# Strassen's scheme on alternate pairs of rows, extended from four gate products to six and to half of the output projection

## The chip, the cores and the metric

The program runs on one core of one Trainium2 chip, with float32 data in and out. The metric is the device time of one execution in microseconds. For the kernel before, three runs gave 1011.74 to 1012.43 us, with a median of 1012.02 us.

## The reference

One decoder layer on x of 256 rows (time steps) by 2048 channels:

```python
u = x @ w_in                                   # 2048 x 17920 weights
a_q, a_f, a_i, a_g, b_q, b_k, b_v, b_g, c_b, c_c, c_x, c_g, m_a, m_b, m_c = split(u)
o_a = rms_norm(hgrn2(a_q, a_f, a_i)) * g * silu(a_g)      # 256 x 1024
o_b = window_attention(b_q, b_k, b_v) * silu(b_g)         # 256 x 1024
o_c = short_conv(c_b, c_c, c_x) * silu(c_g)               # 256 x 1024
merged = sum(sigmoid(m_i) * (o_i @ w_proj_i) for i in "abc")   # each m_i: 256 x 2048
y = merged @ w_out                             # 2048 x 2048
out = layer_norm(alpha * x + y) * ln_g + ln_b
```

What the change touches are the three gate products `m_a`, `m_b`, `m_c` (each x times a 2048 x 2048 part of `w_in`) and `merged @ w_out`.

## The kernel before

**Products in three passes.** Every float32 weight is split into `hi` (a cast to fp32r, ScalarE = ACT, line 114) and `lo` (the rest, VectorE = DVE, line 115); the activations are split in the same way once. A product of a 128 x 128 block of activations with a 128 x 512 block of weights takes three matmuls: hi x hi, lo x hi, hi x lo (`rows`, lines 141 to 145; `product`, lines 663 to 668).

**A plain product.** `gemm(src, xs, 512, "rows")` computes 256 x 512 outputs. Weights come in granules of 1 MB (four k-tiles of 128 rows x 512 columns) through three `raw` buffers; each half granule (128 x 1024) is one `hi` and one `lo` instruction, from pools of four buffers each, and feeds 12 matmuls. A contraction of 2048 has 16 k-tiles and takes 96 matmuls of 128 x 512.

**Gates in pairs of groups.** `gate_pair` (line 656) computes two groups of 512 columns at once, 256 x 1024 outputs, and goes over the contraction in eight pairs of k-tiles, one 1 MB granule each. `PAIRS = (0, 1, 0, 1, 0, 1, 0, 1)` says which pairs are done by the scheme. A plain pair is 2 k-tiles x 2 column groups x 2 row blocks x 3 = 24 matmuls, fed by two splits. In the other pairs the 2 x 2 x 2 block product is done by the Strassen-Winograd scheme in seven products, 21 matmuls. Their operands are sums and differences: of the activations (`sums_of_x`, line 636, once), and of the weights. The latter are made for each such pair: `w` by lines 691 to 693 (128 x 1024 and twice 128 x 512, DVE), then the splits into `hi`, `lo` (128 x 1024), `hi2`, `lo2` (128 x 512) and `hw`, `lw` (128 x 2048). After the last pair one ACT copy (line 721) and eight 128 x 512 DVE additions (lines 722 to 729) combine eight PSUM banks into the outputs, and two sigmoids follow.

**Order of the stages.** Input products with the three mixers, whose steps (`hgrn`, `attn`) are generators in `tasks` that `pump()` advances between half granules; conv(1) to conv(3); then for each of four column groups a plain gate product `rows512(MA + d)` and the first branch's projection `w_proj_hgrn`; then, for the second and the third branch, twice one `gate_pair` and two projections; then `turn` (line 625), which transposes `merged` on TensorE and splits it into the four tiles `ms`; then the output projection `w_out`, three plain groups, each followed by `residual` (line 773: one 128 x 512 line 774 and two line 777 for each row block); last the fourth group, whose split weights are kept (`parts`) and used first for row block 0 and then for row block 1, so that the layer norm of block 0 runs beside the matmuls of block 1.

**Buffers.** Pool `w8` has 12 buffers of 8 KB a partition, given out as `t8`: `xs` takes 4 until the gates end, then come `yc`, the branch outputs `outs[...]` (2 each), `sums` (2), `w`, and, for every second pair of `gate_pair`, `hw` and `lw`; later `ms` (4), the residual input `xres` (2), `lg`, `lbt`, and `h8`, `l8` (the split weights of the first two granules of the last group, two tiles for each granule). Pool `mgp` takes the place of the mixers' pool after `mixers.close()` and holds one `hw` and one `lw`. PSUM has four banks for accumulators and four for other uses; `gate_pair` takes all eight.

**Order on an engine.** Each engine executes its instructions in an order that is fixed when the program is built, and that order isn't the order of the source: an instruction whose operands and buffers are there may be placed ahead of an earlier one that waits. All loads of weights are issued from SyncE's queue, those of `xres`, `lg` and `lbt` from ACT's.

Of the kernel before, what the change touches and what calls it, by code (L numbers as in the profile page):

```python
# [9 lines left out]
F32 = mybir.dt.float32  # L10
# [6 lines left out]
P = 128  # L17
# [25 lines left out]
AI, AG, MA = 0, 2, 4  # L43
# [7 lines left out]
def hybrid_kernel(ctx, tc, a, out):  # L51
# [27 lines left out]
    def f32(ap):  # L79
        return ap.bitcast(F32)  # L80
# [358 lines left out]
    def attn(hf, q, kz, v, gate):  # L439
# [10 lines left out]
        y = t4([P, 4, T], "yb")  # L450
# [64 lines left out]
        outs["b"].append(t8([P, 4, 2, T], "ob", F32R))  # L515
        split_to(outs["b"][hf], y)


    def conv(u):
# [27 lines left out]
        nc.vector.tensor_mul(out=yc[:, 2 * u : 2 * u + 2], in0=y, in1=h)  # L547

# [47 lines left out]
    for w in range(2):  # L596
        r = slice(64 * w, 64 * w + 64)
        nc.scalar.copy(out=kz[0][r, :, w], in_=kr[r])
        nc.vector.tensor_sub(out=kz[1][r, :, w], in0=kr[r], in1=f32(kz[0][r, :, w]))
    for hf in range(2):  # L600
# [14 lines left out]
        tasks.append(attn(hf, q, kz, vb, gate))  # L615
    for u in range(1, 4):
        conv(u)
# [15 lines left out]
    pairs = [p for p in range(KT // 2) if PAIRS[p]]  # L633
    sums = []

    def sums_of_x():
        n = len(pairs)
        xr = rawp.tile([P, n, 2, T], F32, tag="raw", name="xr")
        for i, p in enumerate(pairs):
            nc.sync.dma_start(out=xr[:, i], in_=a["xT"][:, 2 * p : 2 * p + 2])  # L640
        x11, x21 = xr[:, :, 0, :P], xr[:, :, 0, P:]
        x12, x22 = xr[:, :, 1, :P], xr[:, :, 1, P:]
        sx = t8([P, 4, n, P], "sx")
        nc.vector.tensor_add(out=sx[:, 0], in0=x21, in1=x22)
        nc.vector.tensor_sub(out=sx[:, 1], in0=sx[:, 0], in1=x11)
        nc.vector.tensor_sub(out=sx[:, 2], in0=x21, in1=x11)
        nc.vector.tensor_sub(out=sx[:, 3], in0=x12, in1=sx[:, 1])
        yield
        for i in range(0, n, 2):
            dst = t8([P, 2, 4, 2, P], "sums", F32R)  # L650
            sums.append(dst)
            for j in range(2):
                split_to(dst[:, j].rearrange("p s h t -> p s h t"), sx[:, :, i + j])
            yield

    def gate_pair(src):
# [13 lines left out]
        def block(k, t):  # L670
            return [xs[k // 4][:, k % 4, i, t * P : t * P + P] for i in range(2)]
# [3 lines left out]
        for p in range(KT // 2):  # L675
# [28 lines left out]
            i = pairs.index(p)  # L704
            sx = [sums[i // 2][:, i % 2, j] for j in range(4)]
            sx = [[y[:, 0], y[:, 1]] for y in sx]
            k = 2 * p
            end = p == last
            product(p1, block(k, 0), hi[:, :NC], lo[:, :NC], end)
            product(p2, block(k + 1, 0), hi[:, NC:], lo[:, NC:], end)  # L710
            pump()
            product(p6, sx[1], hw[:, 2], lw[:, 2], end)
            product(p7, sx[2], hw[:, 1], lw[:, 1], end)
            product(p5, sx[0], hw[:, 0], lw[:, 0], end)
            product(p3, sx[3], hi2, lo2, end)
            product(p4, block(k + 1, 1), hw[:, 3], lw[:, 3], end)
# [208 lines left out]
```

## Time and profile before

| | us |
|---|---|
| median of three runs | 1012.02 |
| the profiled execution | 1011.4 |
| span of its trace | 1009.6 |
| TensorE (PE) busy | 993.0 (98%) |
| VectorE (DVE) busy | 743.5 (74%) |
| ScalarE (ACT) busy | 541.1 (54%) |
| first of the four `gate_pair` stages starts | 654.5 |
| output projection starts | 907.9 |
| last matmul's result is used | 998.5 |

The profiled execution took 1011.4 us; its trace covers 1009.6 us of that, and 1.8 us lie around it. "Busy" counts the time in which at least one instruction of the engine is recorded; matmuls overlap, so the time that a matmul costs is the distance from its start to the next start, not its recorded duration.

### The profile page before, as it was taken

The numbers are of one execution on the slowest core, as the hardware profiler recorded it, in microseconds if no ns is written. First come the engines' busy times: TensorE is split into PE (matmuls) and PEld (weight loads), VectorE is DVE, ScalarE is ACT, GpSimd is POOL, SyncE is SP. The second block draws the span as 40 slices with busy tenths as digits, with TensorE's granted clock in tenths as the row PEclk, the third lists the DMA queues.
The fourth block names the chain that finished last, engine by engine and source line by source line (L and its number), as shares of the span: only waits on it lengthen the run. The fifth ranks groups of instructions, "written<-read, shape, count | busy, mean of one in ns | idle before, by whom it ended". The sixth has DMA issues, their size and how long they took to land.

```text
span 1009.6 us, 13674 instructions
## 1 busy us (share of the span) xinstructions
PE 993.0 (98%) x5454; PEld 839.3 (83%) x5454; DVE 743.5 (74%) x930; ACT 541.1 (54%) x716; POOL 32.4 (3%) x32
## 2 busy tenths in 40 slices
PE   8999999999999999999999999999999999999995
PEld 5888888888888888888888888888888888887885
DVE  6557889689955777778674554687988889876666
ACT  5545578656654665645554434455555564544341
POOL 1000100210010000000000000000000000000003
PEclk9999999999999999999999999999999999999998
DMA  8755545454455545444456555565655555567442
GB/s 318 256 178 198 187 147 184 151 183 155 168 207 187 188 153 197 163 164 161 167 208 213 204 191 187 205 208 195 216 177 205 208 208 208 183 236 290 173 161 83
DMA packets 30831, 193.67 MB, mean 192 GB/s; under 512 B 3840, under 2 KB 4640, under 8 KB 8752
## 3 DMA queue, kind: packets, MB, share of 16 engines
q1 hardware_dynamic: 28944, 185.90, 52.2%
q10 hardware_dynamic: 1152, 4.72, 1.2%
q0 software_dynamic: 672, 2.20, 0.7%
q8 instruction: 42, 0.69, 0.3%
q14 instruction: 21, 0.17, 0.0%
HBM read 190.68 MB, written 2.12 MB: 191 GB/s over the span
## 4 chain that ended last, share of the span: by engine, by line
PE 97%; DVE 1%; DMA 1%; SPq 0%; ACT 0%; issue 0%
PE acc L151 24%; PE acc L145 13%; PE acc L143 13%; PE acc L144 13%; PE acc L150 12%; PE p L668 5%; PE p L667 5%; PE p L666 5%; DMA raw<-in_w_rows 1%; PE sc L464 1%; PE pvb L507 1%; PE acc L153 1%; PE pT L497 1%; PE lev L390 0%; PE pv L416 0%; PE lev L378 0%
## 5 line engine op out<-in xcount | busy, mean ns | idle before, releaser
L114 ACT CAST hi<-raw 128x1024 fp32r<-128x1024 f32 (+1 forms) x341 | 349.3, 1028 | 348.2 <-PE acc L144 143.4
L115 DVE TENSOR_TENSOR lo<-raw,hi 128x1024 fp32r<-128x1024 f32 (+1 forms) x341 | 404.5, 1194 | 175.0 <-ACT hi L114 173.4
L151 PE MATMUL acc<-xs,hi 128*128 128x512 f32 x1056 | 371.6, 396 | 0.0
L150 PE MATMUL acc<-xs,lo 128*128 128x256 f32 x990 | 278.4, 281 | 0.0
L151 PEld LDWEIGHTS acc<-xs,hi 128*128 128x128 f32 x1056 | 196.9, 188 | 43.5
L150 PEld LDWEIGHTS acc<-xs,lo 128*128 128x128 f32 x990 | 186.8, 189 | 2.3
L143 PE MATMUL acc<-hi,xs 128*128 128x512 f32 (+1 forms) x288 | 110.2, 383 | 2.3 <-ACT hi L114 2.3
L145 PE MATMUL acc<-lo,xs 128*128 128x512 f32 (+1 forms) x288 | 108.8, 379 | 0.4 <-DVE lo L115 0.3
L144 PE MATMUL acc<-hi,xs 128*128 128x512 f32 (+1 forms) x288 | 109.0, 378 | 0.0
L143 PEld LDWEIGHTS acc<-hi,xs 128*128 128x128 f32 x288 | 54.4, 189 | 14.8 <-ACT hi L114 4.4
L145 PEld LDWEIGHTS acc<-lo,xs 128*128 128x128 f32 x288 | 54.1, 188 | 11.5 <-DVE lo L115 1.6
L144 PEld LDWEIGHTS acc<-hi,xs 128*128 128x128 f32 x288 | 54.4, 189 | 9.8
L666 PE MATMUL p<-hi,xs 128*128 128x512 f32 x160 | 62.2, 389 | 0.0
L667 PE MATMUL p<-hi,xs 128*128 128x512 f32 x160 | 62.2, 389 | 0.0
L668 PE MATMUL p<-lo,xs 128*128 128x512 f32 x160 | 62.2, 389 | 0.0
L115 DVE TENSOR_TENSOR lw<-w,hw 128x2048 fp32r<-128x2048 f32 x16 | 36.7, 2293 | 15.0 <-ACT hw L114 15.0
L191 ACT COPY rest<-acc 128x256 f32<-128x256 f32 x66 | 24.1, 372 | 42.2 <-PE acc L151 41.5
L143 PE MATMUL acc<-hi,m 128*128 128x512 f32 (+1 forms) x120 | 45.1, 376 | 1.2 <-ACT hi L114 1.2
L144 PE MATMUL acc<-hi,m 128*128 128x512 f32 (+1 forms) x120 | 45.0, 375 | 0.0
L145 PE MATMUL acc<-lo,m 128*128 128x512 f32 (+1 forms) x120 | 44.9, 376 | 0.1
L667 PEld LDWEIGHTS p<-hi,xs 128*128 128x128 f32 x160 | 30.0, 188 | 6.3
L666 PEld LDWEIGHTS p<-hi,xs 128*128 128x128 f32 x160 | 30.0, 188 | 6.2
(232 smaller groups left out, 1313.1 us busy)
## 6 DMA issues: line engine op xcount, KB each, us to landing
raw<-in_w_cols SPq DMA_DIRECT2D x68, 1024.0 KB, 4.8
raw<-in_w_gate SPq DMA_DIRECT2D x32, 1024.0 KB, 4.8
raw<-in_w_rows SPq DMA_DIRECT2D x28, 1024.0 KB, 4.8
raw<-in_w_out SPq DMA_DIRECT2D x16, 1024.0 KB, 4.9
raw<-in_w_proj_hgrn SPq DMA_DIRECT2D x8, 1024.0 KB, 4.8
raw<-in_w_proj_attn SPq DMA_DIRECT2D x8, 1024.0 KB, 4.8
raw<-in_w_proj_conv SPq DMA_DIRECT2D x8, 1024.0 KB, 4.8
raw<-in_w_rows SPq DMA_DIRECT2D x7, 512.0 KB, 9.2
```

The costliest lines, as they stand in the source:

```text
L114: nc.scalar.copy(out=hi, in_=r)
L115: nc.vector.tensor_sub(out=lo, in0=r, in1=f32(hi))
L143: nc.tensor.matmul(out=acc, lhsT=xk[:, 0, ts], rhs=hi, start=first, stop=False)
L144: nc.tensor.matmul(out=acc, lhsT=xk[:, 1, ts], rhs=hi, start=False, stop=False)
L145: nc.tensor.matmul(out=acc, lhsT=xk[:, 0, ts], rhs=lo, start=False, stop=last)
L150: nc.tensor.matmul(out=acc[:, :T], lhsT=lo, rhs=xk[:, 0], start=False, stop=False)
L151: nc.tensor.matmul(out=acc, lhsT=hi, rhs=xk, start=first, stop=last)
L153: nc.tensor.matmul(out=acc[:, :T], lhsT=lo, rhs=xk[:, 0], start=False, stop=False)
L191: nc.scalar.copy(out=rest[p], in_=acc[p, T:])
L666: nc.tensor.matmul(out=ps, lhsT=x[0], rhs=hi, start=begins, stop=False)
L667: nc.tensor.matmul(out=ps, lhsT=x[1], rhs=hi, start=False, stop=False)
L668: nc.tensor.matmul(out=ps, lhsT=x[0], rhs=lo, start=False, stop=last)
```

## The change

Three places change from plain products to pairs of groups by the scheme. The four plain gate products of the first branch become two calls of `pair_of_groups` (the former `gate_pair`, with the sigmoids moved out and the activations, the sums, the order of the products and the number of spare buffers as arguments). The first two of the four groups of `w_out` become one call, on the transposed `merged`. `turn` makes the sums of `merged` for that. Group 2 of `w_out` stays plain and goes first. `sums_of_x` becomes a task behind the attention. The attention's output stays unsplit in `yb` (one buffer of `w8`), and the outputs of the second and third branch are split ahead of their gates.

```diff
-AI, AG, MA = 0, 2, 4
+AI, AG = 0, 2
...
-        y = t4([P, 4, T], "yb")
+        y = yb[:, 4 * hf : 4 * hf + 4]
...
-        outs["b"].append(t8([P, 4, 2, T], "ob", F32R))
-        split_to(outs["b"][hf], y)
...
+    def block_sums(dst, x11, x12, x21, x22):
+        nc.vector.tensor_add(out=dst[0], in0=x21, in1=x22)
+        nc.vector.tensor_sub(out=dst[1], in0=dst[0], in1=x11)
+        nc.vector.tensor_sub(out=dst[2], in0=x21, in1=x11)
+        nc.vector.tensor_sub(out=dst[3], in0=x12, in1=dst[1])
...
+    yb = t8([P, 8, T], "yb")
...
         tasks.append(attn(hf, q, kz, vb, gate))
+    pairs = [p for p in range(KT // 2) if PAIRS[p]]
+    sums = []
+    tasks.append(sums_of_x())
     for u in range(1, 4):
         conv(u)
     pump(100)
...
-    def turn(m):
+    def turn(m, d):
         dst = t8([P, 4, 2, T], "m", F32R)
         ms.append(dst)
+        if d % 2 == 0:
+            msums.append(t8([P, 2, 4, 2, P], "msums", F32R))
         for i, ps in transpose_pairs([[m[:, t, c * P : c * P + P] for t in range(2)] for c in range(4)], "mT"):
             split_to(dst[:, i : i + 2], ps)
+            if PAIRS[2 * d + i // 2]:
+                raw = mgp.tile([P, 2, T], F32, tag="u", name="mraw")
+                nc.scalar.copy(out=raw, in_=ps)
+                sx = mgp.tile([P, 4, P], F32, tag="one", name="sx")
+                block_sums([sx[:, j] for j in range(4)], raw[:, 0, :P], raw[:, 1, :P], raw[:, 0, P:], raw[:, 1, P:])
+                split_to(msums[d // 2][:, d % 2], sx)
             yield
...
-    def gate_pair(src):
+    def pair_of_groups(src, x, sums, raw_first, spare):
...
-            if pairs.index(p) % 2:
-                hw, lw = t8([P, 4, NC], "hw", F32R), t8([P, 4, NC], "lw", F32R)
-            else:
-                hw = mgp.tile([P, 4, NC], F32R, tag="hw", name="hw")
-                lw = mgp.tile([P, 4, NC], F32R, tag="lw", name="lw")
+            i = pairs.index(p)
+            hw, lw = [t8([P, 4, NC], name, F32R) if i % 2 and n < spare else
+                      mgp.tile([P, 4, NC], F32R, tag=name, name=name) for n, name in enumerate(("hw", "lw"))]
             split_w(w, hw, lw)
...
+            whole = [(p1, block(k, 0), hi[:, :NC], lo[:, :NC]), (p2, block(k + 1, 0), hi[:, NC:], lo[:, NC:])]
+            summed = [(p6, sx[1], hw[:, 2], lw[:, 2]), (p7, sx[2], hw[:, 1], lw[:, 1]), (p5, sx[0], hw[:, 0], lw[:, 0])]
+            rest = [(p3, sx[3], hi2, lo2), (p4, block(k + 1, 1), hw[:, 3], lw[:, 3])]
+            for n, y in enumerate(whole + summed + rest if raw_first or end else summed + rest[::-1] + whole):
+                product(*y, end)
+                if n in (2, 5):
+                    pump()
...
-    for d in range(4):
-        acc = rows512(MA + d)
-        sg = mgp.tile([P, 2, NC], F32, tag="sg", name="sg", bufs=2)
-        for t in range(2):
-            nc.scalar.activation(out=sg[:, t], in_=acc[t], func=AF.Sigmoid)
-        acc = gemm(a["w_proj_hgrn"][d], outs["a"], NC, "rows")
-        for t in range(2):
-            nc.vector.tensor_mul(out=merged[d][:, t], in0=acc[t], in1=sg[:, t])
-    pump(100)
-    for n, (wp, br) in enumerate((("w_proj_attn", "b"), ("w_proj_conv", "c"))):
+    mix = {"b": yb, "c": yc}
+    for n, (wp, br) in enumerate((("w_proj_hgrn", "a"), ("w_proj_attn", "b"), ("w_proj_conv", "c"))):
+        if n:
+            for i in range(2):
+                outs[br].append(t8([P, 4, 2, T], "o" + br, F32R))
+                split_to(outs[br][i], mix[br][:, 4 * i : 4 * i + 4])
         for half in range(2):
-            sg = gate_pair(a["w_gate"][2 * n + half])
...
+            sg = pair_of_groups(a["w_gate"][2 * n + half], xs, sums, n > 0, 2 if n else 1)
+            for y in sg:
+                nc.scalar.activation(out=y, in_=y, func=AF.Sigmoid)
...
-    for n in range(3):
-        acc = gemm(a["w_out"][n], ms, NC, "rows")
+    acc = gemm(a["w_out"][2], ms, NC, "rows")
+    for t in range(2):
+        residual(t, slice(2 * NC, 3 * NC), acc[t])
+    y = pair_of_groups(a["w_out2"][0], ms, msums, False, 0)
+    for n in range(2):
         for t in range(2):
-            residual(t, slice(n * NC, n * NC + NC), acc[t])
+            residual(t, slice(n * NC, n * NC + NC), y[n][:, t])
```

So `spare` is 2 for the second and third branch (as before), 1 for the first (`hw` in two buffers, `lw` in one) and 0 for the output (one `hw`, one `lw`). The weights are the same numbers in another order; as many bytes are loaded.

## Rows read from the trace of the kernel before

**Rows 1.** The page: engine, busy us (share of the span), count of instructions.

```profile
PE 993.0 (98%) x5454; PEld 839.3 (83%) x5454; DVE 743.5 (74%) x930; ACT 541.1 (54%) x716; POOL 32.4 (3%) x32
```

**Rows 2.** The page: chain that ended last, by engine.

```profile
PE 97%; DVE 1%; DMA 1%; SPq 0%; ACT 0%; issue 0%
```

**Rows 3.** PE in order of time, end of the last `gate_pair` (start us, duration).

```profile
878.54 0.39 PE L666 MATMUL p<-hi,xs 128*128 128x512 f32 x1
...
883.07 0.39 PE L668 MATMUL p<-lw,xs 128*128 128x512 f32 x1
883.30 0.39 PE L143 MATMUL acc<-hi,oc 128*128 128x512 f32 x1
```

**Rows 4.** Stretches (us): length, each engine's busy us (instructions), PE clock, DMA.

```profile
500.00:533.00 33.00, 33.00 (x179) 28.40 (x178) 25.46 (x34) 19.07 (x27) 0.00 (x0) 1.00 0.62 218
545.00:654.00 109.00, 109.00 (x483) 90.25 (x482) 56.44 (x50) 47.82 (x49) 0.00 (x0) 1.00 0.55 194
842.20:883.00 40.80, 40.80 (x182) 33.78 (x181) 35.52 (x36) 21.57 (x21) 0.00 (x0) 1.00 0.58 203
883.00:907.90 24.90, 24.90 (x123) 20.54 (x122) 17.55 (x24) 10.70 (x14) 0.00 (x0) 1.00 0.63 233
...
986.90:998.50 11.60, 11.60 (x97) 11.41 (x95) 8.59 (x14) 2.07 (x5) 4.56 (x4) 1.00 0.25 91
```

**Rows 5.** Groups by line and shape: count | busy us, mean ns | idle before.

```profile
L115 DVE TENSOR_TENSOR lo<-raw,hi 128x1024 fp32r<-128x1024 f32 x323 | 392.9, 1223 | 172.9 <-ACT hi L114 171.5
...
L115 DVE TENSOR_TENSOR lw<-w,hw 128x2048 fp32r<-128x2048 f32 x16 | 36.7, 2293 | 15.0 <-ACT hw L114 15.0
L114 ACT CAST hw<-w 128x2048 fp32r<-128x2048 f32 x16 | 30.6, 1913 | 4.6 <-DVE w L693 4.4
...
L691 DVE TENSOR_TENSOR w<-raw 128x1024 f32<-128x1024 f32 x16 | 19.5, 1222 | 0.5 <-DMA raw<-in_w_gate 0.5
...
L115 DVE TENSOR_TENSOR lo<-raw,hi 128x512 fp32r<-128x512 f32 x18 | 12.4, 689 | 2.2 <-ACT hi L114 1.9
...
L692 DVE TENSOR_TENSOR w<-raw,w 128x512 f32<-128x512 f32 x16 | 11.0, 690 | 0.2
...
L430 DVE SCALAR_TENSOR_TENSOR oa<-pv,rs,ga 128x128 f32<-128x128 f32 x16 | 4.3, 344 | 3.6 <-POOL rs L425 3.6
```

**Rows 6.** DVE in order of time, first of the four sums of x.

```profile
515.72 0.69 DVE L644 TENSOR_TENSOR sx<-xr 128x512 f32<-128x512 f32 x1
```

**Rows 7.** DMA issues: queue, count, KB each, median us to landing.

```profile
lbt<-in_ln_b ACTq DMA_DIRECT2D x1, 1024.0 KB, 10.7
```

**Rows 8.** PE in order of time, start of the output projection.

```profile
910.70 1.03 PE L262 MATMUL mT<-ident,merged 128*128 128x128 f32 x8
912.92 0.50 PE L143 MATMUL acc<-hi,m 128*128 128x512 f32 x1 [1.18 <-ACT hi L114]
```

**Rows 9.** DVE in order of time, additions at the end of the last `gate_pair`.

```profile
881.99 1.22 DVE L115 TENSOR_TENSOR lo<-raw,hi 128x1024 fp32r<-128x1024 f32 x1
883.12 0.69 DVE L724 TENSOR_TENSOR sg<-p,u 128x512 f32<-128x512 f32 x1
...
886.11 0.69 DVE L729 TENSOR_TENSOR sg<-p,sg 128x512 f32<-128x512 f32 x1
886.70 2.36 DVE L115 TENSOR_TENSOR lo<-raw,hi 128x1024 fp32r<-128x1024 f32 x2
```

**Rows 10.** DVE in order of time, after the third group of `w_out`.

```profile
977.88 0.74 DVE L777 BATCH_NORM_STATS2 stats<-xres 128x6 f32<-128x256 f32 x2
978.54 0.67 DVE L774 SCALAR_TENSOR_TENSOR xres<-xres,acc 128x512 f32<-128x512 f32 x1
979.13 1.22 DVE L115 TENSOR_TENSOR lo<-raw,hi 128x1024 fp32r<-128x1024 f32 x1
...
987.04 0.69 DVE L774 SCALAR_TENSOR_TENSOR xres<-xres,acc 128x512 f32<-128x512 f32 x1 [6.04 <-PE acc L145]
...
994.94 0.41 DVE L774 SCALAR_TENSOR_TENSOR xres<-xres,acc 128x256 f32<-128x256 f32 x1
```

More of the change, by code (lines that the diff above doesn't have):

```diff
@@ L547, in conv, with sums_of_x @@
         nc.vector.tensor_mul(out=yc[:, 2 * u : 2 * u + 2], in0=y, in1=h)
+    def block_sums(dst, x11, x12, x21, x22):
[3 more added lines that the diff above has]
+        nc.vector.tensor_sub(out=dst[3], in0=x12, in1=dst[1])
+    def sums_of_x():
+        n = len(pairs)
+        xr = rawp.tile([P, n, 2, T], F32, tag="raw", name="xr")
+        for i, p in enumerate(pairs):
+            nc.sync.dma_start(out=xr[:, i], in_=a["xT"][:, 2 * p : 2 * p + 2])
+        sx = t8([P, 4, n, P], "sx")
+        block_sums([sx[:, j] for j in range(4)], xr[:, :, 0, :P], xr[:, :, 1, :P], xr[:, :, 0, P:], xr[:, :, 1, P:])
+        yield
+        for i in range(0, n, 2):
+            dst = t8([P, 2, 4, 2, P], "sums", F32R)
+            sums.append(dst)
+            for j in range(2):
+                split_to(dst[:, j], sx[:, :, i + j])
+            yield
     C = {}
@@ L623, in hybrid_kernel @@
     ms = []
-    def turn(m):
+    msums = []
+    def turn(m, d):
         dst = t8([P, 4, 2, T], "m", F32R)
         ms.append(dst)
+        if d % 2 == 0:
+            msums.append(t8([P, 2, 4, 2, P], "msums", F32R))
         for i, ps in transpose_pairs([[m[:, t, c * P : c * P + P] for t in range(2)] for c in range(4)], "mT"):
             split_to(dst[:, i : i + 2], ps)
-            yield
[L633 to L654, printed above, removed]
-    def gate_pair(src):
+            if PAIRS[2 * d + i // 2]:
[4 more added lines that the diff above has]
+                split_to(msums[d // 2][:, d % 2], sx)
+            yield
+    def pair_of_groups(src, x, sums, raw_first, spare):
         p1, p2, p6, p7 = [accp.tile([P, NC], F32, tag="acc", name=f"p{i}") for i in (1, 2, 6, 7)]
@@ L670, in block @@
         def block(k, t):
-            return [xs[k // 4][:, k % 4, i, t * P : t * P + P] for i in range(2)]
+            return [x[k // 4][:, k % 4, i, t * P : t * P + P] for i in range(2)]
         last = KT // 2 - 1
@@ L697, in gate_pair @@
             split_w(flat[:, 3 * NC :], hi2, lo2)
[L698 to L702 removed]
+            i = pairs.index(p)
+            hw, lw = [t8([P, 4, NC], name, F32R) if i % 2 and n < spare else
+                      mgp.tile([P, 4, NC], F32R, tag=name, name=name) for n, name in enumerate(("hw", "lw"))]
             split_w(w, hw, lw)
[L704 to L706 removed]
+            sx = [[sums[i // 2][:, i % 2, j, m] for m in range(2)] for j in range(4)]
             k = 2 * p
             end = p == last
[L709 to L716, printed above, removed]
[L717 to L718 removed]
+            whole = [(p1, block(k, 0), hi[:, :NC], lo[:, :NC]), (p2, block(k + 1, 0), hi[:, NC:], lo[:, NC:])]
[5 more added lines that the diff above has]
+                    pump()
+        y = [mgp.tile([P, 2, NC], F32, tag="sg", name="sg", bufs=2) for _ in range(2)]
         u = mgp.tile([P, NC], F32, tag="u", name="u")
@@ L744, in hybrid_kernel @@
-    pump(100)
-    for n, (wp, br) in enumerate((("w_proj_attn", "b"), ("w_proj_conv", "c"))):
-        for half in range(2):
-            sg = gate_pair(a["w_gate"][2 * n + half])
-            if br == "c" and not half:
-                for i in range(2):
-                    outs["c"].append(t8([P, 4, 2, T], "oc", F32R))
-                    split_to(outs["c"][i], yc[:, 4 * i : 4 * i + 4])
+        nc.vector.tensor_add(out=y[0][:, 1], in0=p7, in1=u)
+        nc.vector.tensor_add(out=y[1][:, 0], in0=p5, in1=u)
@@ L752, in hybrid_kernel @@
             if br == "c" and half:
-                tasks.extend(turn(merged[d]) for d in range(2))
+                tasks.extend(turn(merged[d], d) for d in range(2))
             for j in range(2):
@@ L903 @@
         "w_out": _weights(i["w_out"][0], NC),
+        "w_out2": _quads(i["w_out"][0][:, : 2 * NC]),
         "lb_param": np.ascontiguousarray(i["lb_param"][0].reshape(8, P).T),
```

32 lines of the change are left out of this document (14 added, 18 removed).

## The prediction

> **What bounds the kernel now.** I read the page's engine list first. PE is busy 98% of the span, DVE 74%, ACT 54% [rows 1]. The reader is to see two candidates there, and that one number settles nothing: overlapping matmuls make a busy PE. The chain of waits, read second, puts 97% on PE [rows 2], so what ends last is a nearly unbroken row of matmuls. Third, PE in order of time: inside a gate pair, and across its end into the next projection, a 128x512 matmul starts every 0.227 us (878.54 to 883.07 us holds 21 of them, 20 steps of 0.2265), although each is recorded with 0.39 [rows 3]. The last matmul of the pair and the first of the projection are 0.23 apart as well: the additions and sigmoids between them cost PE nothing, because halves of the next weights had been split before [rows 9]. So the price of a matmul is 0.227 us, and a matmul less is 0.227 us less, as long as the splits come in time. Fourth, stretches by engine [rows 4]: in the plain first branch DVE is busy 56.4 of 109 us, in a gate pair 35.5 of 40.8. The change moves work from the first kind of stretch to the second. DVE is the engine to watch.
>
> **What is removed.** Two plain groups of contraction 2048 take 2 x 96 = 192 matmuls; a pair of groups takes 4 x 24 + 4 x 21 = 180. Three pairs are new, two in the first branch and one in `w_out`: 36 matmuls fewer, 36 x 0.227 = 8.2 us. The Trainium skill ("TensorE: Matmul & The Clock Gate", Back-to-back issue gap) gives N / 2.4 + 2.5 ns for a warm matmul of N columns, 216 ns for 512; by that the 36 would be worth 7.8 us. The trace has 227 [rows 3], and I use that.
>
> **What DVE gets instead.** Two plain groups are 16 splits, 16 x 1.22 = 19.6 us [rows 5]. A pair of groups is 8 plain splits (9.8), four times 1.22 + 0.69 + 0.69 (`w`) + 1.22 + 0.69 + 2.29 (`lo`, `lo2`, `lw`) = 6.8 each, 27.2 together, and 8 additions (5.5): 42.5 us. So DVE gets 23 us more at each of three places, 69 us. `turn` gets four block sums for each of four tiles; the trace has no 128x128 addition, the nearest is 0.34 us [rows 5], and one split of 0.69: 2.1 us each, 8.3 together. DVE goes to some 820 us. ACT makes the `hi` parts alone, gets less, and starts from 54%: 0, under DVE's cover. Over whole stages that fits: one plain and one scheme row of a pair cost PE 45 x 0.227 = 10.2 us and DVE 2 x 1.22 + 6.8 = 9.3. What counts is where it bunches.
>
> **First branch.** The stage has the shape of the gate stages that run today with PE busy all through (842.2 to 883.0 us, [rows 4]), with one buffer less: `lw` is single. It is free after the twelfth matmul of a scheme row (the new order puts p6, p7, p5, p4 first) and next read 9 + 24 + 2 = 35 matmuls later, 7.9 us; to refill it takes 2.3 us of DVE, with `hw` 4.2 us. I cost it at 0; the cover is the 3.7 us left, and without it each scheme row waits (rival 3). The stage before is now conv(3), where DVE is busy 25.5 of 33 us instead of 56.4 of 109: the entry may be late. Below, 0; above, 3.5 us, if none of the first two rows (2 x 1.22 + 6.5 us of DVE) is ready ahead and only the plain row's 5.45 us of PE covers them. DVE's 7.5 us idle there makes the low end nearer: 0.2 us.
>
> **Moved steps.** `sums_of_x` issues its four loads on SyncE's queue ahead of raw loads, and takes one of three `raw` buffers until its four sums are made. The old program executes its sums from 515.7 us on [rows 6], in conv(3) already, with PE busy 33.00 of 33.00 [rows 4]. So this is no move, 0. Splitting a branch's output ahead of its gates costs 2 x 1.22 us of DVE, twice, beside the two projections before it: 96 matmuls, 21.8 us of PE, over 8 splits and 8 operations of 0.69, 15.3 us of DVE. 0; without that cover up to 2.4 us each. `yb` takes one `w8` buffer more while attention runs. The second half's `q` then has to wait until the first half is done with its `q` and bias, but only its split is late (the products go to small tiles of the mixers' pool), and attention's result is now first read in the second branch: 0.
>
> **`turn`.** From 883.0 to 907.9 us DVE is busy 17.6 of 24.9 [rows 4]; three turns add 6.2 us. That fits by 1 us, so splits may slip: 0 to 2 us, I take 0.2. The wait of 1.18 us at 911.7 to 912.9, where a raw load competes with `xres`, `lg`, `lbt` (10.7 us to land [rows 7]) stays [rows 8].
>
> **The end of the new output pair** is the costly place. Let S be the start of its last scheme row and E = S + 4.8 us its end. The row's p1 can be copied at S + 1.0, the additions start at about S + 1.6 (each 0.60 us after the other, [rows 9]). Behind them now stand four residuals, each 0.60 + 0.66 us [rows 10]: 8 x 0.60 + 4 x 1.26 = 9.8 us of DVE, of which it can do some 2.6 in the 3.2 us before E, as products arrive. It is done at E + 7.2. At today's gate ends only the additions, then a split, follow [rows 9]: six additions from 883.12 went ahead of a split whose `hi` was ready, so I expect additions and residuals ahead of splits here too. What is late next is `lo` of group 3's weights, and they are used at double rate, since row block 0 goes first: half a granule is 6 matmuls, 1.36 us. Which are split before E? `w8` holds `ms` 4, `msums` 1 (the other is free), `xres` 2, `lg`, `lbt`, and the last `w`, until its `lw` is made. (That can begin when the scheme row before has done its p4, 2.7 us into a row that starts 4.8 + 5.4 + 4.8 = 15 us before E, at E - 12.3, and takes 4.2 us: E - 8.) That leaves two buffers for granule 0, one more for granule 1's `h8`; its `l8` must wait for `msums`, which p3 reads until E - 0.5. So PE has granule 0, 12 matmuls and two more with `hi` alone: until E + 3.2. Granule 1's first `lo` ends at E + 7.2 + 1.2 = E + 8.4. The gap is 5.2 us. PE can be given row block 1's matmuls on granule 0 meanwhile, 2 x 12 of 256 columns at 0.12 us (96 in 11.6 us [rows 4]), 2.9 us; that PE's order bends so is seen today: eight transposes stand together [rows 8], though the source has 12 matmuls between the first four and the last four; those waited for `hi`. Left over: 2.3 us. Ends: 0, if the splits go between the additions, as one did [rows 9, 10]; 5.2, if nothing is pulled ahead. I take 2.3. The layer norm of block 0 (987.0 to 994.9 us, 8 us of DVE beside 11.6 of PE) keeps its cover even with 8.7 us of PE left.
>
> A rule that speaks against the change: DVE instructions here start closer than they are long, 0.60 against 0.69 [rows 9], and with starts 0.69 apart the block of 9.8 us would be 8 x 0.69 + 4 x 1.5 = 11.5 and the gap 1.7 longer. The Trainium skill ("VectorE: DVE Perf Modes", Terms, DRAIN) says that the next operation can't issue until the pipe is empty. The trace does not agree for these shapes, so I keep 0.60.
>
> **Sum.** 1011.4 (the profiled execution: span 1009.6 and 1.8 around it) - 8.2 + 2.3 + 0.2 + 0.2 = 1005.9 us. The median of the runs is 0.6 above the profiled one: **1006.5 us**. Less than 0.2% (2 us) can't be told from no change here.
>
> **Rivals.** *1. Everything hidden.* Splits of granules 1 and 2 slip between additions; 1011.4 - 8.2 + 0.6 = 1003.8. For it: a split did stand among the additions [rows 9] and one ahead of the statistics [rows 10]. Against: 9.8 us of DVE and four more halves (4.6 us) don't fit in the 10.9 us of row block 0 without delaying something. Chance 0.22. *2. The gap in full, and its echo.* 5.2 us, plus the layer norm of block 0 pushed into block 1's, or the 1.7 above: 1011.4 - 8.2 + 5.2 + 0.4 to 2 + 0.6 = 1009.4 to 1011. For it: the buffer count. Chance 0.2, a fifth of it within 0.2% of before. *3. Slower: the single buffers.* In 12 scheme rows (8 of the first branch, 4 of the output) `lw`, and in the output `hw` too, has one buffer. If DVE makes `w`, `hw`, `lw` in one chain only after the release, 2.6 + 1.9 + 2.3, with the next plain row's two splits (2.4) among it, that is 9.2 us against 7.9 of cover: 1.3 us a row, 16 us, 1011.4 - 8.2 + 16 + 0.6 = 1020. It decides against the change from 8.2 / 12 = 0.7 us a row. For it: DVE has only 0.9 us free in 10.2. Against: `w` can be made earlier, as its own buffer comes free with the old `lw`; only 4.2 us have to fit. Chance 0.13: 0.05 slower, 0.05 the same, 0.03 still faster.
>
> **How the numbers follow.** Likeliest, 0.45: a part of the gap, 1004.5 to 1008.5, at 1006.5. Rival 1 gives 1003 to 1004.5, rival 2 up to 1011. A range of 1003 to 1010.5 leaves out most of rival 3, and the far end of rival 2. Faster by over 0.2% (below 1010.0): 0.45 + 0.22 + 0.16 + 0.03 = 0.86; within: 0.04 + 0.05 = 0.09; slower: 0.05.
>
> **What would show it.** Right: 5418 PE instructions instead of 5454; 180 matmuls in 40.8 us in the first branch's pairs, without idle; DVE near 820 us; after the output pair's last product PE idle some 2 us, ended by a `lo` or `l` of line 115, with matmuls of 256 columns of row block 1 ahead of it. Wrong: PE idle in scheme rows, ended by `hw` or `lw` (rival 3); no idle at E (rival 1); 5 us there (rival 2). A wait for `qb` in attention's second half, or for `sums` at the first branch's entry, would be a step that I costed at nothing.

## The result and the profile after

The changed kernel takes 1004.99 us (median of four runs, 1004.12 to 1005.54); the kernel before took 1011.90 beside it (1011.74 to 1012.43). The ratio is 0.9930, with a 95% interval of 0.9913 to 0.9947: faster, by 6.9 us. Predicted were 1006.5, within 1003.0 to 1010.5. The profiled execution took 1005.54 us, the longest of the four, with a span of 1003.6. Against the profile of before that is 6.0 us of span, against 6.9 in the medians, and the rows below account for the 6.0. (One run of `raw_first_residuals_late`, further down, had a mean granted clock of 0.655 and took 1407.97 us; it is left out of that kernel's times, and as it was the profiled one, no row of that kernel is read.)

The page after, its engine line and its chain (to [rows 1, 2]):

```profile
PE 985.9 (98%) x5418; PEld 833.0 (83%) x5418; DVE 808.5 (81%) x1022; ACT 562.7 (56%) x735; POOL 33.0 (3%) x32
...
PE 92%; DVE 5%; DMA 1%; issue 1%; ACT 1%; SPq 0%; DVEq 0%; ACTq 0%
```

The 36 matmuls are gone (5454 to 5418). DVE has 65 us more and is still no bound on average. But its part of the chain went from 1% to 5%, so the engine that the prediction watched does end some waits now. Where it does not, the stretches show (length, then busy us of PE, PEld, DVE, ACT, POOL, then granted clock, DMA share and GB/s; the first new pair, a pair that was one before, the projection that now holds the larger `turn`, and the new output pair):

```profile
525.76:566.71 40.95, 40.95 (x181) 33.70 (x180) 35.57 (x35) 23.54 (x24) 0.00 (x0) 1.00 0.58 202
...
838.71:879.50 40.79, 40.79 (x181) 33.78 (x180) 35.52 (x37) 21.86 (x21) 0.00 (x0) 1.00 0.57 200
879.51:904.21 24.70, 24.70 (x121) 20.27 (x120) 23.26 (x39) 16.04 (x22) 0.00 (x0) 1.00 0.50 173
...
926.97:968.44 41.47, 41.10 (x182) 33.72 (x180) 38.59 (x42) 23.61 (x23) 0.00 (x0) 1.00 0.60 213
```

The first new pair looks as the last pair did before [rows 4]: PE without a break, DVE at 35.6 us. The projection with `turn` has 23.3 of 24.7 us of DVE and still no idle PE. Only in the output pair is PE's busy time below the length, by 0.37 us.

A ledger of the two traces, by the start of the first matmul of each stage: up to the first input product +0.36; the attention's last transposes +1.14; the first gate to the output projection 383.72 to 378.45, of which four plain groups became two pairs, -5.44; the output stage 90.26 to 87.64, -2.62; behind the last matmul +0.39. The output stage holds -2.72 (12 matmuls), -1.58 (two waits of before are gone, 1.35 us from start to start at 911.5 us [rows 8] and 0.23 at 913.7), +0.53 (a wait in its second scheme row) and +1.00 (the gap at E: 1.12 us from 974.84 to 975.96, where 0.12 is the usual step behind a matmul of 256 columns). With small change the sum is the 6.0 us. The +0.36 at the start is scatter: at 18 us, behind work that is the same in all these kernels, the ten other traces read here are between 1.1 us earlier and 0.6 us later than that of before, the changed kernel's 0.3 later, and they keep this distance up to the attention.

**The gap at E.** PE after the output pair's last product (E = 968.44):

```profile
968.21 0.39 PE L679 MATMUL p<-lw,m 128*128 128x512 f32 x1
968.44 0.39 PE L143 MATMUL acc<-h,m 128*128 128x512 f32 x1
...
971.38 0.39 PE L144 MATMUL acc<-h,m 128*128 128x512 f32 x1
971.61 0.28 PE L143 MATMUL acc<-h,m 128*128 128x256 f32 x1
...
974.84 0.28 PE L144 MATMUL acc<-h,m 128*128 128x256 f32 x1
975.96 0.50 PE L145 MATMUL acc<-l,m 128*128 128x512 f32 x1 [0.84 <-DVE l L115]
976.30 0.40 PE L143 MATMUL acc<-h,m 128*128 128x512 f32 x1
```

and DVE beside it, from the first addition on (to [rows 9, 10]):

```profile
965.54 0.69 DVE L727 TENSOR_TENSOR sg<-p,one 128x512 f32<-128x512 f32 x1
...
970.32 0.68 DVE L734 TENSOR_TENSOR sg<-p,sg 128x512 f32<-128x512 f32 x1
970.92 0.75 DVE L776 BATCH_NORM_STATS2 stats<-xres 128x6 f32<-128x256 f32 x2
971.58 1.29 DVE L773 SCALAR_TENSOR_TENSOR xres<-xres,sg 128x512 f32<-128x512 f32 x2
972.77 1.41 DVE L776 BATCH_NORM_STATS2 stats<-xres 128x6 f32<-128x256 f32 x4
974.09 0.68 DVE L773 SCALAR_TENSOR_TENSOR xres<-xres,sg 128x512 f32<-128x512 f32 x1
974.68 1.23 DVE L115 TENSOR_TENSOR l<-raw,h 128x1024 fp32r<-128x1024 f32 x1
```

14 matmuls of 512 columns, then 28 of row block 1 with 256 columns pulled ahead, then a wait for a split `l` that stands behind the additions and residuals.

**Behind the last matmul.** DVE at the last residual of row block 1, before and after (the last matmul starts at 998.24 and at 991.85 us):

```profile
998.55 0.42 DVE L774 SCALAR_TENSOR_TENSOR xres<-xres,acc 128x256 f32<-128x256 f32 x1 [2.74 <-PE acc L145]
...
989.35 3.12 DVE L799 SCALAR_TENSOR_TENSOR xres<-xres,rstd,lbt 128x512 f32<-128x512 f32 x3
992.73 0.40 DVE L773 SCALAR_TENSOR_TENSOR xres<-xres,acc 128x256 f32<-128x256 f32 x1
```

Before, DVE waited 2.74 us for PE there, with the layer norm of block 0 done. Now that layer norm's last instructions (L799) end at 992.47, and the residual starts 0.88 us behind the last matmul's start instead of 0.32. In the seven traces with the output pair and its residuals in this place, 11.76 to 12.08 us lie behind the start of the last matmul; in the other four (before, `gates_only`, `residuals_late`, `both_late`) 11.23 to 11.38.

**The attention, where no wait was foreseen.** PE and DVE before, at its last softmax:

```profile
483.45 0.40 PE L151 MATMUL acc<-xs,hi 128*128 128x512 f32 x1
483.96 1.06 PE L497 MATMUL pT<-ident,s 128*128 128x128 f32 x8
...
482.18 0.16 DVE L486 TENSOR_TENSOR den<-den,es 128x4 f32<-128x4 f32 x1 [2.13 <-ACT s L484]
482.59 1.22 DVE L488 TENSOR_TENSOR s<-s,den 128x1024 f32<-128x1024 f32 x1
```

and after:

```profile
484.17 0.39 PE L151 MATMUL acc<-xs,hi 128*128 128x512 f32 x1
485.81 1.06 PE L497 MATMUL pT<-ident,s 128*128 128x128 f32 x8 [1.26 <-DVE s L488]
...
482.23 0.68 DVE L549 TENSOR_TENSOR sx<-sx,xr 128x512 f32<-128x512 f32 x1
482.83 0.68 DVE L550 TENSOR_TENSOR sx<-xr 128x512 f32<-128x512 f32 x1
483.44 0.68 DVE L551 TENSOR_TENSOR sx<-xr,sx 128x512 f32<-128x512 f32 x1
484.04 0.15 DVE L486 TENSOR_TENSOR den<-den,es 128x4 f32<-128x4 f32 x1
484.44 1.22 DVE L488 TENSOR_TENSOR s<-s,den 128x1024 f32<-128x1024 f32 x1
```

Three of the four sums of x, 1.8 us of DVE that nobody needs before 525, stand right ahead of the softmax's division, for which PE waits. Before, DVE was idle there and the sums came at 515.72 [rows 6].

**A second wait in the output pair.** PE's wait between 938 and 945 us (who waited on what: us in total, times, longest):

```profile
PE p L679 <- DVE lw L115: 0.4, 1, 0.4
```

DVE is the late one, because its work for the pair starts late. The chain of `w`, `hw` and `lw` begins with the weights of the first scheme row, and DVE makes their first `w` at 924.06, when they land, 2.9 us ahead of the pair's first matmul. The stretch ahead of that, and the loads of weights issued between 912 and 921 us (count, KB each, median us to landing), after and before:

```profile
908.00:922.00 14.00, 14.00 (x65) 11.49 (x65) 8.56 (x12) 7.00 (x10) 0.00 (x0) 1.00 1.00 404
...
raw<-in_w_out SPq DMA_DIRECT2D x3, 1024.0 KB, 7.6
...
raw<-in_w_out SPq DMA_DIRECT2D x3, 1024.0 KB, 4.9
```

The DMA engines are busy all the time there, at 404 GB/s, and a load takes 7.6 us. Six traces with the same work in this pair show that its start sets the wait: the first `w` leads the pair by 3.9 us in `both_late`, 3.2 in `sums_late`, 2.9 in the changed kernel, 2.6 in `one_buffer`, 2.5 in `output_only` and 2.4 in `residuals_late`, and the wait, from start to start, is 0, 0.23, 0.53, 0.85, 0.89 and 1.00 us. DVE also has the residual of group 2 there (L773 at 928.80 and 932.60, with its statistics at 931.93 and 933.79), 2.5 us; but the second pair of the second and of the third branch has four instructions of 128x512 in that place, 2.4 us, and no wait. What makes the loads land late no run tried.

### The profile page after: what moved, and what is told of

Read it like the earlier page. It is cut to its first block, busy times and chain, and to the rows that moved or that the text cites. A ratio compares the mean times of both kernels' runs of the same rounds, so it can differ in the third digit from the quotient of the medians.

```text
span 1003.6 us, 13714 instructions
## 1 busy us (share of the span) xinstructions
PE 985.9 (98%) x5418; PEld 833.0 (83%) x5418; DVE 808.5 (81%) x1022; ACT 562.7 (56%) x735; POOL 33.0 (3%) x32
## 4 chain that ended last, share of the span: by engine, by line
PE 92%; DVE 5%; DMA 1%; issue 1%; ACT 1%; SPq 0%; DVEq 0%; ACTq 0%
PE acc L151 24%; PE acc L150 11%; PE acc L143 9%; PE p L677 9%; PE acc L145 9%; PE p L679 9%; PE p L678 9%; PE acc L144 9%; DVE lo L115 1%; PE acc L153 1%; PE sc L464 1%; PE pvb L507 1%; DMA raw<-in_w_rows 1%; DVE xres L799 1%; PE pT L497 1%
## 5 line engine op out<-in xcount | busy, mean ns | idle before, releaser
L677 PE MATMUL p<-hi,xs 128*128 128x512 f32 x240 | 93.4, 389 | 0.0
L678 PE MATMUL p<-hi,xs 128*128 128x512 f32 x240 | 93.4, 389 | 0.0
L679 PE MATMUL p<-lo,xs 128*128 128x512 f32 x240 | 93.4, 389 | 0.0
L115 DVE TENSOR_TENSOR lw<-w,hw 128x2048 fp32r<-128x2048 f32 x28 | 64.2, 2292 | 22.2 <-ACT hw L114 20.8
L143 PE MATMUL acc<-hi,xs 128*128 128x512 f32 (+1 forms) x160 | 60.6, 379 | 2.3 <-ACT hi L114 2.3
L114 ACT CAST hw<-w 128x2048 fp32r<-128x2048 f32 x28 | 53.6, 1913 | 11.4 <-DVE w L704 11.2
L145 PE MATMUL acc<-lo,xs 128*128 128x512 f32 (+1 forms) x160 | 59.5, 374 | 0.0
L144 PE MATMUL acc<-hi,xs 128*128 128x512 f32 (+1 forms) x160 | 59.4, 371 | 0.0
L679 PEld LDWEIGHTS p<-lo,xs 128*128 128x128 f32 x240 | 45.1, 188 | 9.4
L678 PEld LDWEIGHTS p<-hi,xs 128*128 128x128 f32 x240 | 45.1, 188 | 9.3
L677 PEld LDWEIGHTS p<-hi,xs 128*128 128x128 f32 x240 | 45.0, 188 | 9.3
L143 PEld LDWEIGHTS acc<-hi,xs 128*128 128x128 f32 x160 | 30.4, 190 | 10.0 <-ACT hi L114 4.5
L702 DVE TENSOR_TENSOR w<-raw 128x1024 f32<-128x1024 f32 x28 | 34.2, 1221 | 1.2 <-DMA raw<-in_w_gate 0.9
L144 PEld LDWEIGHTS acc<-hi,xs 128*128 128x128 f32 x160 | 30.6, 191 | 4.9
```

The lines of the kernel that those rows point to most:

```text
L114: nc.scalar.copy(out=hi, in_=r)
L115: nc.vector.tensor_sub(out=lo, in0=r, in1=f32(hi))
L143: nc.tensor.matmul(out=acc, lhsT=xk[:, 0, ts], rhs=hi, start=first, stop=False)
L144: nc.tensor.matmul(out=acc, lhsT=xk[:, 1, ts], rhs=hi, start=False, stop=False)
L145: nc.tensor.matmul(out=acc, lhsT=xk[:, 0, ts], rhs=lo, start=False, stop=last)
L677: nc.tensor.matmul(out=ps, lhsT=x[0], rhs=hi, start=begins, stop=False)
```

## The experiments

All are the changed kernel with the edits named; times are medians, ratios are to the kernel before (1011.78 to 1011.81 us in the shared runs).

**`matmuls_back`: the 36 matmuls again.**

```diff
             for n, y in enumerate(whole + summed + rest if raw_first or end else summed + rest[::-1] + whole):
+                if y is rest[0] and not raw_first:
+                    product(*y, False)
                 product(*y, end)
```

> The changed kernel with the third product of every scheme row of the three new pairs done twice (its result is added twice), which puts the 36 saved matmuls back and leaves DVE, ACT and the loads as they are. Theory A: PE sets the time, a matmul costs 0.227 us. Then 8.2 us come back, less a few tenths of the waits that the longer rows cover (0.5 us at 943 us): 1012.6 to 1013.2, above the kernel before by what the change's waits cost. Rival B: DVE, now 81% busy, sets the time in the new pairs; then the matmuls are free in its shadow and the time rises by less than 4 us.

1012.74 us (10 runs, 1011.8 to 1013.22), ratio 1.0009 [1.0000, 1.0019]: +7.75. The first new pair went from 40.72 us (first to last start) to 43.44 with 12 matmuls more, 0.227 each. With the sums, additions and residuals kept but the matmuls back, nothing of the gain is left, so the gain is the matmuls.

**`gates_only` and `output_only`: one place at a time.** `gates_only` has three plain groups of `w_out` and the old `turn`; `output_only` has the first branch's four plain gate products and old loop.

```diff
-    acc = gemm(a["w_out"][2], ms, NC, "rows")
...
-    y = pair_of_groups(a["w_out2"][0], ms, msums, False, 0)
-    for n in range(2):
+    for n in range(3):
+        acc = gemm(a["w_out"][n], ms, NC, "rows")
```

```diff
+    for d in range(4):
+        acc = rows512(MA + d)
...
-            sg = pair_of_groups(a["w_gate"][2 * n + half], xs, sums, n > 0, 2 if n else 1)
+            sg = pair_of_groups(a["w_gate"][2 * n + half], xs, sums, True, 2)
```

> The changed kernel without the output part: the four groups of the output projection plain as before, no sums in the turning of merged. Theory A: 24 matmuls fewer at 0.227 us are 5.4 us; the waits of the output pair (0.5 to 1.1 us at 943 us, 0.9 us at 975 us) go, the one in attention (1.1 us more than before) stays. 1011.8 - 5.4 + 1.1 = 1007.5, between 1007 and 1008.2. Rival B: the first branch, at 86% DVE with one lw buffer less, gives part of its gain back: then more than 1008.5, with PE waits between 526 and 651 us. Parts: this and the output part alone should add up to the whole change but for the wait in attention, which both have.

> The changed kernel with the four plain gate products of the first branch as before; the output pair, the later splits and the place of the sums stay. Theory A: 12 matmuls fewer are 2.7 us; against that stand the wait in attention (1.1), those of the output pair (0.5 to 1.1 and 0.9), and the wait of 1.2 us at 912 us, which the change lost, may or may not return. 1011.8 - 2.7 + 1.1 + 0.5 + 0.9 - 1.2 = 1010.4, and 1011.6 with the wait at 912. So the output part alone hardly pays. Rival B: it pays its whole 2.7 us, the waits being those of the first branch's pressure on the buffers: 1009.1 or less.

`gates_only` 1007.08 us (4 runs), ratio 0.9953 [0.9938, 0.9968]; `output_only` 1009.74 (10 runs), 0.9983 [0.9973, 0.9992]: -4.7 and -2.0, together -6.7 of the 6.9, although both carry the wait at 484 us (1.2 and 1.4 us from start to start, where before had 0.5). The first came as theory A had it, the second between its two (1010.4, and 1009.1 or less). The old wait at the start of the output projection is back in `gates_only`, and not in `output_only`. In `gates_only`, PE and ACT at that place:

```profile
905.77 1.03 PE L262 MATMUL mT<-ident,merged 128*128 128x128 f32 x8
907.99 0.50 PE L143 MATMUL acc<-hi,m 128*128 128x512 f32 x1 [1.18 <-ACT hi L114]
...
906.40 0.58 ACT L87 CAST m<-mT 128x512 fp32r<-128x512 f32 x1 [8.06 <-PE mT L262]
906.88 1.05 ACT L114 CAST hi<-raw 128x1024 fp32r<-128x1024 f32 x1
```

ACT had stood idle for 8.06 us before the transposes' cast, with the `hi` that PE then waits for behind it in its order. It is the second half of a granule whose first half ACT had cast at 893.88, so its load had landed long before. In the changed kernel the last turn's transposes stand apart, four and four, and no step between PE's starts is over 0.32 us from 904 to 917 us:

```profile
906.93 0.60 PE L262 MATMUL mT<-ident,merged 128*128 128x128 f32 x4
...
910.14 0.60 PE L262 MATMUL mT<-ident,merged 128*128 128x128 f32 x4
```

So the wait belonged to ACT's order around `turn`, and not to the loads of `xres`, `lg` and `lbt` as the prediction had it.

**`sums_late`: the sums of x behind the convolutions.**

```diff
-    tasks.append(sums_of_x())
     for u in range(1, 4):
         conv(u)
+    tasks.append(sums_of_x())
```

> The changed kernel (1005.0 us) with the task that makes the sums of x put behind conv(3) in the source, where it stood before. In the changed kernel PE waits 1.4 us at 484.2 us (0.3 us in the kernel before) ahead of the last four transposes of attention, and the four sums of x and the first of their splits stand on DVE and ACT between that block's maxima and its division. Theory A: these cause the wait. Then the wait goes back to about 0.3 us, and the time is 1.1 us shorter: 1003.9 us. Rival B: the wait comes from attention itself, whose second half got its q and its bias later (the split of q at 390.8 us instead of 361 to 376 us); then the wait stays at 1.4 us and the time at 1005.0. Rival C: the sums, now later, delay the first scheme row of the first branch; then 1.4 us leave attention and as much appears between 526 and 540 us.

1004.07 us (5 runs, 1003.03 to 1005.04), ratio 0.9924 [0.9911, 0.9936]. The wait at 484 us is gone (482.44 to 482.85, 0.41 from start to start), so the sums' place caused it. The first branch's first pair takes 40.91 us, so rival C is out. The median fell 0.9, within the scatter of the runs; the 1.1 us rest on the trace. The wait in the output pair's second scheme row is down to 0.23 us, as the weights landed earlier there.

**`residuals_late`: the output pair's four residuals behind the splits of the last group.**

```diff
     y = pair_of_groups(a["w_out2"][0], ms, msums, False, 0)
-    for n in range(2):
-        for t in range(2):
-            residual(t, slice(n * NC, n * NC + NC), y[n][:, t])
     parts = []
...
                 parts.append(split_w(raw[:, s], h8[:, s], l8[:, s]))
+    for n in range(2):
+        for t in range(2):
+            residual(t, slice(n * NC, n * NC + NC), y[n][:, t])
```

> The changed kernel with the four residuals of the output pair put behind the splits of the last group's weights in the source. In the changed kernel PE waits 0.9 us at 975 us for the first lo part of granule 1, which stands behind nine additions and four residuals on DVE. Theory A (the step of the prediction): the residuals are what delays it. Then that lo part comes about 4 us earlier, PE has no wait there, no matmuls of row block 1 are pulled ahead, and the time is 0.5 to 0.9 us shorter, less what the layer norm of row block 0 loses (it starts when the residuals are done): 1004.1 to 1005.0. Rival B: the buffer (granule 1's lo needs the tile of the activations' sums, free only at the pair's end) or the load of granule 1 delays it: then the wait stays near 0.9 us, at another place or not, and the time at 1005.0.

1002.71 us (4 runs, 1002.51 to 1004.80), ratio 0.9916 [0.9903, 0.9930]. DVE, where `l` now follows the additions:

```profile
971.23 0.68 DVE L734 TENSOR_TENSOR sg<-p,sg 128x512 f32<-128x512 f32 x1
971.83 2.35 DVE L115 TENSOR_TENSOR l<-raw,h 128x1024 fp32r<-128x1024 f32 x2
```

`l` starts at E + 2.5 instead of E + 6.2, PE pulls only 6 matmuls of 256 columns ahead, and the gap is gone. The median fell by 2.3. The profiled run is the longest of its four (1004.80), and its trace is 0.75 us shorter than the changed kernel's: the gap gives 1.1 with the slow step behind it, the end behind the last matmul 0.5, while the first branch starts 0.4 later and the wait in the second scheme row is 0.5 longer. The rest of the 2.3 was not seen.

**`both_late`: both moves.**

> The changed kernel with both moves at once, the sums of x behind conv(3) and the residuals of the output pair behind the splits of the last group. Alone they gave 1004.07 and 1002.71 (1004.99 without). Theory A: they mend waits at different places, 484 and 975 us, and add up: 1001.5 to 1002.5, with no PE wait over 0.2 us after the first 20 us. Rival B: what one gains, the other loses, as DVE has little idle time from the first branch on (the wait at 943 us grew to 1.0 us in the second): 1002.7 or more.

1001.90 us (4 runs, 1001.13 to 1003.20), ratio 0.9904 [0.9889, 0.9919]: the two add up, 3.1 us below the changed kernel and the best version here. From 20 us on, no two matmuls of it start more than 0.42 us apart up to the last one; the attention and the output pair:

```profile
480.00:490.00 10.00, 9.98 (x58) 8.53 (x57) 7.12 (x11) 6.82 (x14) 0.00 (x0) 1.00 0.62 210
926.50:968.00 41.50, 41.50 (x185) 34.37 (x184) 38.70 (x43) 23.91 (x25) 0.00 (x0) 1.00 0.61 219
```

**`one_buffer`: one `hw` and one `lw` in all seven pairs.**

```diff
-            sg = pair_of_groups(a["w_gate"][2 * n + half], xs, sums, n > 0, 2 if n else 1)
+            sg = pair_of_groups(a["w_gate"][2 * n + half], xs, sums, n > 0, 0)
```

> The changed kernel with one hw and one lw buffer in all seven pairs of groups (spare = 0), that is in 24 scheme rows of six pairs where there were two or one and a half. Theory A: the 7.9 us of PE between the release of a buffer and its next reading cover the 4.2 us of refilling, so the rows start without a wait: 1005.0 to 1006.5. Rival B (the third rival of the prediction): the refilling chain shows, 0.7 us or more for each scheme row that loses a buffer, 12 rows of the second and third branch with full loss: 1013 us or more.

1005.11 us (4 runs), ratio 0.9935 [0.9921, 0.9948]: nothing. No wait of PE in any branch's pair, those in the old order of products included; the waits at 484, 943 and E stay. The 1.3 us a row of rival 3 did not show.

**`raw_first`: the old order of the seven products everywhere.**

```diff
-            sg = pair_of_groups(a["w_gate"][2 * n + half], xs, sums, n > 0, 2 if n else 1)
+            sg = pair_of_groups(a["w_gate"][2 * n + half], xs, sums, True, 2 if n else 1)
...
-    y = pair_of_groups(a["w_out2"][0], ms, msums, False, 0)
+    y = pair_of_groups(a["w_out2"][0], ms, msums, True, 0)
```

> The changed kernel with the former order of the seven products (the unsummed weights first) in the three new pairs too. Then hw and lw are read until a row's end and free only there, 30 matmuls or 6.8 us ahead of their next reading instead of 33 and 35; refilling both takes 4.2 us. Theory A: cover still suffices, the time stays at 1004.5 to 1006. Rival B: the order is what keeps the single buffers off the path; without it each of the 12 rows waits 0.5 us or more: 1011 or more.

1009.26 us (6 runs, 1007.26 to 1011.47), ratio 0.9975 [0.9962, 0.9988]: 4.3 us worse, and not as any of the theories had it. The scheme rows have hardly a wait (one of 0.2 us). The loss is at E and just behind it. ACT, DVE and PE of that kernel, and the stretch from 979.17 to 982.54 us:

```profile
964.97 2.00 ACT L114 CAST h<-raw 128x1024 fp32r<-128x1024 f32 x2 [3.09 <-DVE lw L115]
966.87 0.57 ACT L726 COPY one<-p 128x512 f32<-128x512 f32 x1
...
967.48 0.69 DVE L727 TENSOR_TENSOR sg<-p,one 128x512 f32<-128x512 f32 x1 [2.55 <-ACT one L726]
...
976.63 1.22 DVE L115 TENSOR_TENSOR l<-raw,h 128x1024 fp32r<-128x1024 f32 x1
...
974.48 0.28 PE L144 MATMUL acc<-h,m 128*128 128x256 f32 x1
977.91 0.50 PE L145 MATMUL acc<-l,m 128*128 128x512 f32 x1 [3.15 <-DVE l L115]
...
979.17:982.54 3.37, 3.37 (x11) 2.79 (x10) 3.37 (x4) 0.00 (x0) 0.00 (x0) 0.51 0.03 5
```

`hw` and `lw` come free only at the end of the row before, so the last `lw` ends at 964.93. ACT waits 3.09 us for that to cast `h` of the last group, and the copy that starts the additions stands behind this cast on ACT. Additions and residuals begin 2.3 us later against E, `l` follows them, and PE waits 3.2 us instead of 0.8. Then, after 1.3 us of work, the granted clock is half for 3.4 us, and the eleven steps from 979.17 on take 1.6 us more than at full clock. The trace is 3.9 us longer than the changed kernel's, and 2.3 for the longer gap and 1.6 for the clock are all of it.

**`raw_first_residuals_late`: the old order, with the residuals moved as in `residuals_late`.**

> The changed kernel with the old order of the seven products in the three new pairs, as in raw_first (1009.26 us), and with the four residuals of the output pair recorded behind the two splits, as in residuals_late (1002.71 us). Nothing is left out. Theory A: what the old order cost (4.3 us) is all at the end of the output pair, where DVE's additions and residuals stood ahead of the split of granule 1; with the residuals behind that split the gap of 3.4 us at about 974 closes to under 1 us and the time comes to 1002.7 to 1005.5 us. Theory B: the late release of hw and lw in the old order costs in the scheme rows or through w's buffer wherever the residuals stand: the time stays at 1006.5 us or above.

1004.36 us (three runs, 1004.20 to 1005.42), ratio 0.9928 [0.9912, 0.9945]. With the residuals out of the way the old order comes back by 4.9 us, into theory A's span: its loss did run through what stands ahead of `l` at E. That the half clock went with the gap is likely, but no trace of this kernel shows it. The mean granted clocks of these three runs are 0.995 to 0.997, those of the six of `raw_first` 0.991 to 0.995. Not all of the loss came back, though: the move gains 2.3 us in the new order too, and 1.7 us remain between this kernel and `residuals_late`, with intervals that overlap. Where these lie no trace here shows.

**`vector_more`: how near is DVE to its limit?**

```diff
+            for _ in range(1 if raw_first else 2):
-            nc.vector.tensor_sub(out=w[:, 0:2], in0=raw[:, 0:1].to_broadcast([P, 2, NC]), in1=raw[:, 1::2])
+                nc.vector.tensor_sub(out=w[:, 0:2], in0=raw[:, 0:1].to_broadcast([P, 2, NC]), in1=raw[:, 1::2])
```

> The changed kernel with one subtraction of 128x1024 elements on DVE (the first of the three in w) made twice in each of the 12 scheme rows of the three new pairs; the second writes what the first wrote. 12 x 1.13 us = 13.6 us more of DVE, no matmul more. Theory A (PE sets the time in the pairs, DVE's spare time in the projections between them takes up what is more): DVE's busy time goes to about 822 us, the branches' new pairs keep 40.6 to 41.0 us each, waits are found in the output pair and behind it alone, 1005 to 1007.5 us. Theory B (DVE is at its limit in a scheme row, so that what is more is paid): 0.5 to 1.1 us a row, 1011 to 1018 us, with PE waiting on w or its split in the branches' pairs.

1011.14 us (10 runs, 1009.69 to 1012.50), ratio 0.9996 [0.9986, 1.0005]: +6.1, the lower edge of theory B's time, but not at B's places. The first branch's first pair, the output pair, and PE there (profiled run 1009.69):

```profile
525.51:566.90 41.39, 41.38 (x181) 33.63 (x180) 38.07 (x38) 23.85 (x24) 0.00 (x0) 1.00 0.55 193
...
927.11:970.96 43.85, 41.64 (x181) 33.45 (x180) 41.41 (x44) 23.36 (x22) 0.00 (x0) 1.00 0.58 210
...
935.26 0.50 PE L679 MATMUL p<-lw,msums 128*128 128x512 f32 x1 [2.09 <-DVE lw L115]
...
979.63 0.50 PE L145 MATMUL acc<-l,m 128*128 128x512 f32 x1 [1.99 <-DVE l L115]
```

The eight scheme rows of the first branch take 9.0 us more of DVE for 0.4 us of time. The output pair takes four, 4.5 us, and pays 2.4 in the pair (41.47 to 43.85) and 1.2 in the group behind it. So DVE has slack in the branches and none at the start of the output pair. There the first `w` begins 3.3 us ahead of the pair, when its weights land, and the residual of group 2 now stands ahead of the first `lw`, which starts 5.8 us into the pair instead of 2.75. What the late weights and the residual each cost no run tells apart. The span is 3.7 us longer; the profiled run is the shortest of ten, and the rest of the 6.1 was not seen.

## Why the prediction was right, and where its steps failed

**The matmuls (right).** 8.2 us was the term, by 0.227 us each. -5.44 in the branch and -2.72 in the output are 8.16, and `matmuls_back` gave 7.75 back. The Trainium skill ("TensorE: Matmul & The Clock Gate", Back-to-back issue gap) gives 216 ns by its formula, by an estimate 2.59 us for the 12 matmuls more of a pair, where 2.72 was measured; the same section's sustained 131 ns would be, by the same estimate, 1.6. The measured 227 ns decide against both.

**DVE (right in kind).** 820 us were forecast, 808.5 came: the terms were added with recorded durations, while instructions start 0.60 us apart that are recorded with 0.69. The 128x128 sums of `turn` take 0.29 us, not 0.34.

**First branch, single buffers, `yb`, branch splits (right).** All were costed at 0, and 0 is what the trace shows: 180 matmuls in 40.95 us, no wait at the entry (525.53, 525.76), none for `qb`. Rival 3 fell with `one_buffer`. Its arithmetic took `w` to be made only after the release; `vector_more` shows that 1.13 us more a row fit in the branches.

**"The end of the new output pair", 2.3 us (mechanism right, size 1.00).** The wait is where it was put, ended by `l`, with PE filling in row block 1. Additions and residuals ahead of `l` took 9.14 us instead of 9.8, since the last statistics slipped behind `l`. The split ended at E + 7.5 instead of E + 8.4, and PE pulled 28 matmuls ahead instead of 24. `residuals_late` closed the gap by taking away exactly what was said to stand in front. The spacing of 0.60 against the DRAIN rule held here again: nine steps from 965.54 to 970.92 are 0.598 each. The same page of the Trainium skill ("VectorE: DVE Perf Modes", Two Vector instructions with no wait between them) lets an instruction start before the one ahead has finished, unless it is held, and the trace agrees with that section.

**"The layer norm of block 0 keeps its cover" (failed, +0.39).** The prediction had 8.7 us of PE left beside 8 us of DVE. PE had pulled 32 of block 1's 96 matmuls ahead, 28 in the gap and 4 a little later, so 64 of 0.12 us were left, 7.7 us, and DVE was late for the last residual by 0.56 us. With the residuals moved 6 are pulled ahead, and the loss is gone (`residuals_late`, `both_late`).

**"Moved steps: so this is no move, 0" (failed, +1.14).** The argument was that the sums already ran at 515.7 us, in conv(3). It took their place in the old trace for a property of the work, but it followed from their place in the source. As a task behind the attention they were ready at 478 to 484 us and went ahead of a softmax that PE was about to wait for. `sums_late` removes the wait by the place alone.

**"`turn`: the wait of 1.18 us stays" (failed, -1.58 with the smaller one behind it).** It was put down to a load that competes with `xres`, `lg` and `lbt`; it was ACT's order, which the new `turn` and output changed. This gain and the loss in the attention nearly cancel, so that the sum came out better than its parts.

**What was missed.** The wait of 0.53 us in the output pair's second scheme row, where the weights of the first one land late, and +0.36 ahead of the first matmul of the inputs, which is scatter. By the trace's own sum the profiled execution comes to 1011.4 - 6.0 = 1005.4, where 1005.9 was the sum predicted. The steps were further off than that: 1.3 too much for the gap, 1.6 for waits that went and 0.4 for the entry and `turn`, against 1.1, 0.5 and 0.75 of time not foreseen and 0.3 of small steps. These errors nearly cancel, so the closeness of the sum is in part luck; the 8.2 us of the matmuls and the place of the gap are not.

## What to carry to other kernels

Price a removed matmul by its distance from start to start, and then read what the scheme gives DVE stage by stage: the same 1.13 us was nearly free in the branches and dear in the output pair, where DVE starts late, when its weights land, and has a residual to do besides. Where a list of ready work orders an engine, work that is needed late must be put late in the source: sums 40 us early cost 1.1 us, residuals ahead of splits 1.0 in the gap and 0.4 at the end, and moving both gave 3.1 in the medians. A wait in the old trace is only carried over to the new one after asking which engine's order made it.

## What the runs showed of the hardware

A wait of PE costs a little more than its idle time: the first matmul behind one is recorded with 0.50 us instead of 0.39, and the next starts 0.34 us after it instead of 0.227 (975.96 and 976.30 in the changed kernel), 0.11 more for each wait. A longer wait can cost more: in `raw_first` TensorE, idle for 3.15 us, worked 1.3 us at full clock, and then its granted clock was 0.51 over 3.37 us, nearly all of it at half (1.2 of 2.4 GHz). A matmul of 512 columns started every 0.427 us there (980.83 to 981.26 us) instead of 0.227. Behind waits of 0.84 us (the changed kernel) and 1.99 us (`vector_more`) at the same place it stayed full. One trace shows the fall there; three others (the changed kernel, `residuals_late`, `vector_more`) have 3.4 us at half clock from 11.5 to 12.1 us on, near PE's waits for the first loads.

And lateness of a load is felt where the work behind it has no lead: of the six kernels compared above, PE waited 1.00 us in the output pair where the first `w` led it by 2.4 us, and not at all where it led by 3.9.
